# When to transpose the queries of a banded attention: four bursts at the group's begin, or one each two steps

## The chip, the core and the metric

One core of one Trainium2 chip runs the whole layer in a single launch. The metric is the device time in microseconds, the median over runs of the same program. TensorE (PE) does the matrix products and, as products with an identity, the transposes; VectorE (DVE) and ScalarE (ACT) do elementwise work and empty PSUM; GpSimd (POOL) and SyncE (SP) issue most of the DMAs.

## The reference

One layer of a decoder trunk: 256 tokens, width 2048, in float32. Two attentions run in parallel on the same normalized input, are gated and merged, and a gated feed-forward network with a short convolution follows. What matters here is the second attention, a banded one with 32 query heads of 64 columns and 4 key/value heads:

```python
s = jnp.einsum('bqhgd,bnkhd->bhgnqk', q, kb).astype(jnp.float32) * SWA_HEAD_DIM ** -0.5
...
s = jnp.where(mask[None, None, None], s + bias[None], -jnp.inf)
m = jnp.maximum(jnp.max(s, axis=-1), sink)
p = jnp.exp(s - m[..., None])
denom = jnp.sum(p, axis=-1) + jnp.exp(sink - m)
p = (p / denom[..., None]).astype(vb.dtype)
out = jnp.einsum('bhgnqk,bnkhd->bnqhgd', p, vb)
```

## The kernel before, in words

Products of float32 are made of three products of a high and a low part (`mm3`, lines 163 to 165). A weight chunk of 128 x 1024 is loaded by SP, ScalarE casts it into the high part (`whi`, line 137), VectorE subtracts to get the low part (`wlo`, line 138); up to four chunks of high and low parts are in store (`RING`), and three raw ones (`RAW`).

The big products run one after another (`gemm`, line 167). One of 512 columns takes eight chunks, with twelve matmuls of 512 columns each. After every chunk `tick()` runs the functions that were put down for that **step** with `at(step, f)`. So the attention is laid between the chunks of the products: a step is a chunk's twelve matmuls plus what was put down for it. The framework's scheduler then orders each engine's instructions with this order as the priority, and may move one later when it expects its inputs later.

The attention is cut into four **groups** (one for each key/value head, `g`) and 16 **units** of two query heads (`u`, four in a group). Group g's queries come out of one big product; group g is worked on while the next product runs. With b the first step of the group:

- `swa_q` (line 405) empties the product's two PSUM tiles into the query tiles `qx` (high and low part of each head side by side, lines 219 and 220). There are two such tiles, both used by one group.
- `swa_qT` (line 414) transposes a unit's queries: four 128 x 128 transposes on TensorE into one PSUM tile `xp` (line 420), copied by ScalarE to the tile `x2..` (line 423; the profile shows it as `x`; three buffers).
- `swa_unit` (line 433) puts down the unit's other steps, with t0 = b + 2 + 2i for unit i of the group: scores (`s`, lines 450 and 452) and their bias and maxima on VectorE (454 to 456) at t0; the exponentials on ScalarE (472) and the normalization, half on VectorE (484) and half on ScalarE (482), at t0 + 1; the transposes `pt` of the probabilities (430), emptied into `pth` by ScalarE (216) and `ptl` by VectorE (217), at t0 + 3; the product `po` with the values (498 to 501), emptied by ScalarE (503) and VectorE (506), at t0 + 4.

So in a running group a step holds either the scores of one unit and the `po` of an earlier one, or two `pt`. PSUM has eight banks: four for the big products (`pacc`), two for scores (`pss`) and two (`pst`) that `xp`, `pt`, `po` and, at the beginning, the key transposes `kt` take in turn:

```python
pst = ctx.enter_context(tc.tile_pool(name="pst", bufs=2, space=PS))
```

A tile of `pst` can be written only when the tile two before it in that pool has been emptied.

Of the kernel before, what the change touches and what calls it, by code (L numbers as in the profile page):

```python
# [41 lines left out]
def trunk_layer(ctx, tc, x, x_cols_in, conv_cols_in, g_mix_post, g_ffn_post, w_in, w_q, w_kv,  # L42
# [16 lines left out]
    def sb(pl, shape, name, dt=F32, tag=None, bufs=None):  # L59
        return pl.tile(shape, dt, name=name, tag=tag or name, **({"bufs": bufs} if bufs else {}))  # L60
# [84 lines left out]
    def at(t, *fs):  # L145
        steps[max(t, now[0])].extend(fs)
# [20 lines left out]
    def gemm(xh, xl, w, k0, nk, c0, n, split=False, extra=None, ps=None):  # L167

        kc = 1024 // n if n in (256, 512) else 2
        acc = new_acc("g", ps)  # L170
        todo = []
        cuts = list(range(0, nk, kc)) + [nk]
        for ci, (k, ke) in enumerate(zip(cuts[:-1], cuts[1:])):
            kk = ke - k
            src = w[(k0 + k) * P:(k0 + k + kk) * P, c0:c0 + n].rearrange("(a p) n -> p a n", p=P)
            hi, lo = wchunk(src, [kk, n], *(extra or {}).get(ci, ()))
            for j in range(kk):
                kt = k + j
                wh, wl = hi[:, j * n:(j + 1) * n], lo[:, j * n:(j + 1) * n]
                for t in range(NT):  # L180
                    def go(kt=kt, t=t, wh=wh, wl=wl):
                        mm3(acc[t][:, :n], xh(k0 + kt)[:, t * P:(t + 1) * P],
                            xl(k0 + kt)[:, t * P:(t + 1) * P], wh, wl, kt == 0, kt == nk - 1)
                    if split and t == 1:
                        todo.append(go)
                    else:
                        go()
            tick()
        return acc, todo
# [215 lines left out]
    def swa_q(g, acc):  # L405

        qx_of[g] = []
        for t in range(NT):
            q = sb(p1, [P, 8, 2, 64], f"qx{g}_{t}", F32R, tag="qx", bufs=2)
            a3 = acc[t].rearrange("p (a b) -> p a b", b=64)  # L410
            split_to(q[:, :, 0, :], q[:, :, 1, :], a3, r1s[:, t:t + 1])
            qx_of[g].append(q)

    def swa_qT(u):

        qx, i = qx_of[u // 4], u % 4
        pt = pst.tile([P, 512], F32R, name=f"xp{u}", tag="t")
        for j in range(2):
            for t in range(NT):
                pe.transpose(pt[:, (j * 2 + t) * P:(j * 2 + t + 1) * P],  # L420
                             qx[t][:, 2 * i + j, :, :].rearrange("p a b -> p (a b)"), ident_r)
        xt = sb(p1, [P, 512], f"x2{u}", F32R, tag="x2", bufs=3)
        act.copy(xt, pt.bitcast(F32))
        xs_of[u] = xt
# [91 lines left out]
    for g in range(4):  # L516
        acc = gemm(XH, XL, w_in, 0, KT, C_QS + 512 * g, 512)[0] if g else acc_q0
        swa_q(g, acc)
        b = now[0]
        for i in range(4):  # L520
            at(b + 1 + i // 2, lambda u=4 * g + i: swa_qT(u))
            swa_unit(4 * g + i, b + 2 + 2 * i)


# [235 lines left out]
    b = now[0] + 42  # L760
# [11 lines left out]
    for j in range(4):  # L772
        acc, _ = gemm(XH, XL, w_in, 0, KT, C_GA + 512 * j, 512)
        for t in range(NT):
            g = stg(f"ta{j}_{t}")
# [46 lines left out]
    for j in range(4):  # L822
        ld = merge_loads(j)
        acc, _ = gemm(AH, AL, wo_a, 0, KT, 512 * j, 512)
        for t in range(NT):
            a, b = ld[t]
# [354 lines left out]
```

## Time and profile before

| what | value |
|---|---|
| time before, median of 3 runs | 1485.88 us (1485.74 to 1486.16) |
| the profiled execution's own time | 1485.58 us |
| its span in the profile | 1483.8 us |
| granted TensorE clock, mean | 0.999 |
| transposes of the queries | 64 on TensorE, from 59.4 to 165.5 us |

The times of the profile count from the span's start. Between the span and the execution's own time lie 1.8 us that the profile does not show. An entry such as `PE xp L420 <- ACT x L423: 0.3, 2, 0.2` reads: TensorE's instruction of line 420, which writes xp, waited for ScalarE's instruction of line 423, which writes x; 0.3 us in total, two times, 0.2 us at the longest. In rows in order of time, the first number is the start, the second the duration, and the brackets at the end hold the idle time before and who ended it.

### The profile page before, as it was taken

To read this page: it belongs to the slowest core of one execution; us is meant where nothing else is said; L and a number is where in the kernel's file an instruction comes from. 1 tells how busy PE (TensorE), PEld (TensorE's weight loads), DVE (VectorE), ACT (ScalarE), POOL (GpSimd) and SP (SyncE) were. 2 spreads that over 40 slices of the span, in tenths; PEclk is the share of its full clock that TensorE was granted. 3 is DMA by queue.
4 is the path that set the end of the run, shared out by engine and by line. 5 is a ranking of instruction groups with operands and counts; after the bars stand their busy time and mean duration, and the time that the engine had idled before them with its cause. 6 is when DMAs were issued, how large, how long until landed. Compare 5 with 4: busy or idle time off the path is not lost.

```text
span 1483.8 us, 21178 instructions
## 1 busy us (share of the span) xinstructions
PE 1470.5 (99%) x7797; PEld 1261.1 (85%) x7797; DVE 979.3 (66%) x1711; ACT 806.3 (54%) x1336; POOL 57.0 (4%) x97
## 2 busy tenths in 40 slices
PE   9999999999999999999999999999999999999997
PEld 7888888888899988888888888888888888888887
DVE  7688884445677765555698777675444676677555
ACT  7588874434555554444566555554444555555443
POOL 0122200000000001000000000000000000000000
PEclk9999999999999999999999999999999999999999
DMA  9776566666655559656656666665566666665663
GB/s 306 206 170 175 137 198 187 208 209 206 185 157 157 167 160 334 225 185 213 197 178 176 199 191 178 196 191 190 190 194 198 187 187 193 188 188 185 195 197 114
DMA packets 162323, 285.52 MB, mean 192 GB/s; under 512 B 18555, under 2 KB 34844, under 8 KB 162092
## 3 DMA queue, kind: packets, MB, share of 16 engines
q1 hardware_dynamic: 157436, 268.39, 58.3%
q0 software_dynamic: 4784, 15.78, 4.5%
q8 instruction: 61, 1.00, 0.3%
q14 instruction: 42, 0.34, 0.1%
HBM read 277.79 MB, written 6.34 MB: 191 GB/s over the span
## 4 chain that ended last, share of the span: by engine, by line
PE 94%; DVE 3%; ACT 2%; issue 1%; DMA 0%; SPq 0%; DVEq 0%
PE accg L164 18%; PE accg L165 18%; PE accg L163 18%; PE ua L997 10%; PE ub L997 10%; PE ua L1001 5%; PE ub L1001 5%; PE mpo L748 1%; DVE wlo L138 1%; PE ms L714 1%; ACT p L472 1%; PE qn L677 1%; PE qn L679 1%; PE qn L678 1%; PE acckv L164 0%
## 5 line engine op out<-in xcount | busy, mean ns | idle before, releaser
L138 DVE TENSOR_TENSOR wlo<-raw,whi 128x1024 fp32r<-128x1024 f32 (+2 forms) x501 | 609.2, 1217 | 419.6 <-ACT whi L137 417.8
L137 ACT CAST whi<-raw 128x1024 fp32r<-128x1024 f32 (+2 forms) x501 | 523.2, 1046 | 547.0 <-PE accg L165 303.8
L163 PE MATMUL accg<-whi,bhl 128*128 128x512 f32 (+1 forms) x608 | 230.8, 380 | 0.0
L165 PE MATMUL accg<-whi,bhl 128*128 128x512 f32 (+1 forms) x608 | 230.1, 378 | 0.0
L164 PE MATMUL accg<-wlo,bhl 128*128 128x512 f32 (+1 forms) x608 | 230.0, 378 | 0.0
L163 PE MATMUL accg<-whi,ahl 128*128 128x512 f32 (+1 forms) x544 | 212.8, 391 | 0.0
L164 PE MATMUL accg<-wlo,ahl 128*128 128x512 f32 (+1 forms) x544 | 210.4, 387 | 0.0
L165 PE MATMUL accg<-whi,ahl 128*128 128x512 f32 (+1 forms) x544 | 210.1, 386 | 0.0
L997 PE MATMUL ub<-ahl,whi 128*128 128x512 f32 x640 | 160.3, 392 | 0.0
L997 PE MATMUL ua<-ahl,whi 128*128 128x512 f32 x640 | 160.2, 392 | 0.0
L997 PEld LDWEIGHTS ua<-ahl,whi 128*128 128x128 f32 x640 | 115.7, 189 | 21.1
L997 PEld LDWEIGHTS ub<-ahl,whi 128*128 128x128 f32 x640 | 115.6, 189 | 20.9
L165 PEld LDWEIGHTS accg<-whi,bhl 128*128 128x128 f32 x608 | 114.4, 188 | 21.2
L163 PEld LDWEIGHTS accg<-whi,bhl 128*128 128x128 f32 x608 | 114.4, 188 | 21.0
L164 PEld LDWEIGHTS accg<-wlo,bhl 128*128 128x128 f32 x608 | 114.4, 188 | 20.9
L165 PEld LDWEIGHTS accg<-whi,ahl 128*128 128x128 f32 x544 | 102.2, 188 | 20.3
L163 PEld LDWEIGHTS accg<-whi,ahl 128*128 128x128 f32 x544 | 102.3, 188 | 17.9
L164 PEld LDWEIGHTS accg<-wlo,ahl 128*128 128x128 f32 x544 | 102.3, 188 | 17.6
L1001 PEld LDWEIGHTS ub<-ahl,wlo 128*128 128x128 f32 x640 | 86.3, 191 | 5.6
L1001 PEld LDWEIGHTS ua<-ahl,wlo 128*128 128x128 f32 x640 | 86.0, 191 | 5.5
L1001 PE MATMUL ub<-ahl,wlo 128*128 128x256 f32 x640 | 88.0, 282 | 0.0
L1001 PE MATMUL ua<-ahl,wlo 128*128 128x256 f32 x640 | 87.9, 282 | 0.0
(331 smaller groups left out, 1617.6 us busy)
## 6 DMA issues: line engine op xcount, KB each, us to landing
raw<-in_ffn_w_up_dram SPq DMA_DIRECT2D x176, 512.0 KB, 4.5
raw<-in_w_in_dram SPq DMA_DIRECT2D x111, 512.0 KB, 4.5
raw<-in_ffn_w_down_dram SPq DMA_DIRECT2D x88, 512.0 KB, 3.8
raw<-in_w_o_swa_dram SPq DMA_DIRECT2D x32, 512.0 KB, 4.1
raw<-in_w_o_mla_dram SPq DMA_DIRECT2D x32, 512.0 KB, 4.7
raw<-in_w_out_dram SPq DMA_DIRECT2D x32, 512.0 KB, 4.2
raw<-in_mla_w_q_up_dram SPq DMA_DIRECT2D x48, 128.0 KB, 3.0
bias<-strip POOLq DMA_DIRECT2D x16, 256.0 KB, 4.1
```

Of the source, the lines that this page charges most:

```text
L137: act.copy(hi[:, :n], raw[:, :n])
L138: vec.tensor_tensor(lo[:, :n], raw[:, :n], hi[:, :n].bitcast(F32), op=ALU.subtract)
L163: pe.matmul(o, ah, bh, start=start, stop=False)
L164: pe.matmul(o, ah, bl, start=False, stop=False)
L165: pe.matmul(o, al, bh, start=False, stop=stop)
L472: act.activation(pb[:, i, a:b], pb[:, i, a:b], AF.Exp, bias=st["nm"][:, i, t:t + 1], accum_out=st["sm"][:, i, t:t + 1])
L677: pe.matmul(o, wh, ch(k), start=k == 0, stop=False)
L678: pe.matmul(o, wh, cl(k), start=False, stop=False)
L679: pe.matmul(o, wl, ch(k), start=False, stop=k == nk - 1)
L714: pe.matmul(o, w, v_, start=n == 0, stop=False)
L997: pe.matmul(acc[i], hi[:, c], hn[p][:, j * 512:(j + 1) * 512], start=p + j == 0, stop=stop)
L1001: pe.matmul(acc[i][:, 0:256], lo[:, c], hn[p][:, j * 512:j * 512 + 256], start=False, stop=False)
```

## The change

The query transposes of a group's four units are put down at the steps b + 1, b + 2, b + 4 and b + 6 in place of b + 1, b + 1, b + 2 and b + 2. The scores of the four units stay at b + 2, b + 4, b + 6 and b + 8.

```diff
         swa_q(g, acc)
         b = now[0]
         for i in range(4):
-            at(b + 1 + i // 2, lambda u=4 * g + i: swa_qT(u))
+            at(b + max(1, 2 * i), lambda u=4 * g + i: swa_qT(u))
             swa_unit(4 * g + i, b + 2 + 2 * i)
```

No instruction is added or removed. What stands on TensorE, in order, from the end of group 1 to the begin of group 2 in the two built programs (g12 are twelve matmuls of the big product; the numbers are units):

```
before  s7 g12 pt6 g9  xp8 g1 xp9 g2 po6 s8 xp10 g10 xp11 g6 pt7 g8 po7 s9 g12 pt8 g12 po8 s10
after   s7 g12 pt6 g11 xp8 g1 po6 s8 xp9 g12 pt7 g12 po7 s9 xp10 g12 pt8 g12 po8 s10 xp11
```

## The prediction

> **What bounds the kernel now.** I read the page first, then the answer for the tile xp (the transposed queries), then the waits of the stretch in which these transposes stand (52 to 212 us), then busy time by stretch, and last the instructions in order of time.
>
> ```profile
> PE 1470.5 (99%) x7797; PEld 1261.1 (85%) x7797; DVE 979.3 (66%) x1711; ACT 806.3 (54%) x1336; POOL 57.0 (4%) x97
> PE 94%; DVE 3%; ACT 2%; issue 1%; DMA 0%; SPq 0%; DVEq 0%
> ```
>
> TensorE is busy for 99% of the span and carries 94% of the chain that ended last. So only what TensorE waits for, or does in a costlier order, counts.
>
> ```profile
> L420 PE MATMUL xp<-ident_r,qx x64: 222/248/306, 59.4 to 165.5; 128*128 128x128 f32 x64
> L423 ACT CAST x<-xp x16: 565/587/603, 60.2 to 165.8; 128x512 fp32r<-128x512 f32 x16
> ```
>
> The 64 transposes are 16 bursts of four, each with one copy by ScalarE (0.59 us), all before 166 us. The built programs say how far the change reaches: on each engine the orders are the same up to the first burst and again from about 215 us on; the DMA queue of SP keeps its order throughout, and no instruction is added or dropped. So everything is decided in some 155 us of 1484, where TensorE waits this much:
>
> ```profile
> PE pt L430 <- ACT pth L216: 0.4, 1, 0.4
> PE xp L420 <- ACT x L423: 0.3, 2, 0.2
> PE cqT L550 <- DVE ptl L217: 0.3, 1, 0.3
> PE po L498 <- DVE ptl L217: 0.3, 1, 0.3
> PE xp L420 <- DVE ptl L217: 0.2, 1, 0.2
> ```
>
> That is 1.5 us in all. Its helpers are less at ease. In these two stretches (length; PE, PEld, DVE, ACT, POOL busy with counts; clock; DMA) VectorE has next to no idle time:
>
> ```profile
> 80.00:90.00 10.00, 10.00 (x55) 8.53 (x54) 9.91 (x32) 8.56 (x22) 2.34 (x3) 1.00 0.70 197
> 150.00:160.00 10.00, 10.00 (x54) 8.18 (x53) 9.86 (x30) 8.79 (x23) 3.88 (x6) 1.00 0.55 142
> ```
>
> **The waits that go.** A burst writes one of the two pst banks; the transposes of the probabilities (pt, two per unit) and the output products (po) use the same two. Before, steps 1 and 2 of a group ask for seven banks, later steps for one or two; after, every step asks for at most three. In the built program the second bursts of groups 2 and 3 (xp9, xp13), which wait 0.3 for a copy, move behind a unit's scores. And po4, which waits 0.3 because xp7 had pushed pt4 to within five products of it, gets a full step of twelve again. One wait grows: xp4, which stands twelve products behind pt2 and waits 0.2 for VectorE to empty its bank, now stands eleven behind it, so 0.2 more. Together 0.3 + 0.3 - 0.2 = 0.4 us. The other two waits belong to unit 14 and to the latent product, and stay.
>
> **What the place of a burst costs.** Two bursts in order of time, the first inside the big product, the second right behind a unit's scores, and then two products behind scores with no burst:
>
> ```profile
> 60.57 0.40 PE L163 MATMUL accg<-whi,ahl 128*128 128x512 f32 x1
> 60.85 0.53 PE L420 MATMUL xp<-ident_r,qx 128*128 128x128 f32 x4
> 61.22 0.47 PE L164 MATMUL accg<-wlo,ahl 128*128 128x512 f32 x1
> 61.52 0.39 PE L165 MATMUL accg<-whi,ahl 128*128 128x512 f32 x1
> ...
> 64.52 0.45 PE L420 MATMUL xp<-ident_r,qx 128*128 128x128 f32 x4
> 64.81 0.46 PE L163 MATMUL accg<-whi,ahl 128*128 128x512 f32 x1
> 65.11 0.40 PE L164 MATMUL accg<-wlo,ahl 128*128 128x512 f32 x1
> ...
> 72.88 0.39 PE L163 MATMUL accg<-whi,ahl 128*128 128x512 f32 x1
> 73.11 0.40 PE L164 MATMUL accg<-wlo,ahl 128*128 128x512 f32 x1
> ```
>
> By starts, a product takes 0.23 us. The burst alone takes TensorE from 60.80 (60.57 + 0.23) to 61.29 (61.52 - 0.23), 0.49 us; the one behind scores from 64.52 to 64.88, 0.36 us. So a place inside the product costs 0.13 us more: one switch in and one out, where the scores' own switch back is free (73.11 - 72.88 is 0.23). Before, ten runs of bursts stand inside the product or before a pt (xp1, xp3, xp4 with xp5, xp7, xp8, xp9, xp11, xp12, xp13, xp15); after, three (xp4, xp8, xp12, which wait for pt's bank and land one product ahead of po). Seven fewer at 0.13 give 0.9 us. Group 1 before also has pt3, pt4 and the scores of unit 5 cut in two by products or by po3; three such cuts, gone, at the same 0.13 give 0.4 us. The gain is 0.4 + 0.9 + 0.4 = 1.7 us; with the cuts free and no wait gone, 0.9; with xp4's wait gone as well, 2.1.
>
> The Trainium skill (TensorE: Matmul & The Clock Gate, Back-to-back issue gap) speaks against the 1.3 us of places: the spacing depends on the matmul's own columns, N / 2.4 + 2.5 ns, about 216 ns for 512, and names no cost of a switch. By it the gain would be the waits alone, 0.4 us. The rows above have 0.30 us between two products behind a burst and 0.23 elsewhere, so I go by the rows.
>
> **What becomes late.** In-order queues of ScalarE and VectorE are rearranged, and four things come near TensorE's need.
>
> First, units 5 and 9. Here is the end of a group before: ScalarE's normalization (L482) of unit 5, its share of the next queries (L219), and the transposes that need the former.
>
> ```profile
> 115.08 0.80 ACT L482 ACTIVATE p<-p,sm 128x128 f32<-128x128 f32 x2
> 116.20 1.27 ACT L219 ACTIVATE qx<-accg,r1s 128x512 fp32r<-128x512 f32 x2
> 116.53 0.82 PE L430 MATMUL pt<-ident,p 128*128 128x128 f32 x6
> ```
>
> After, ScalarE's queue has the copy of xp7, both L219, and only then L482. L219 needs the product's end, so L482 ends at 116.20 + 1.27 + 0.80 = 118.27. The pt of unit 5 now stands five products later; its second half, which needs L482, is due at 116.53 + 5 x 0.23 + 0.29 = 117.95. TensorE waits 0.3 to 0.4; for units 5 and 9, 0.7 us. If the queue ahead is late there, more; nothing excludes up to twice that.
>
> Second, units 3, 7 and 11, whose pt comes much sooner behind the scores of the next unit than before. The rows of unit 12's scores and unit 11's normalization:
>
> ```profile
> 161.02 1.05 ACT L137 CAST whi<-raw 128x1024 fp32r<-128x1024 f32 x1
> 161.53 0.28 PE L450 MATMUL s<-kx,x 128*128 128x256 f32 x1
> 163.58 1.22 DVE L138 TENSOR_TENSOR wlo<-raw,whi 128x1024 fp32r<-128x1024 f32 x1
> 165.32 0.42 DVE L506 TENSOR_TENSOR o<-po,cr 64x256 f32<-64x256 f32 x1
> 165.77 0.55 DVE L484 TENSOR_SCALAR p<-p,sm 128x128 f32<-128x128 f32 x2
> 167.03 0.82 PE L430 MATMUL pt<-ident,p 128*128 128x128 f32 x6
> ```
>
> Before, VectorE's normalization ends 4.79 us after the scores' start (166.32 - 161.53), and pt starts 5.50 after. After, pt is due at 0.70 (scores) + 0.36 (burst) + 0.07 + 12 x 0.23 = 3.9. But the order also puts the two weight splits, 1.05 us on ScalarE and 1.22 on VectorE, behind the normalization, which brings its end to 3.6 to 4.0. So the wait lies between nothing and 0.9 (4.79 - 3.9); I take 0.1, 0.3 for three.
>
> Third, the group's tail. The copy of xp15 (0.59) is new ahead of the casts of unit 13, and TensorE itself comes 0.36 later. po13 waits already (0.44 between these two where a product of 320 columns takes 0.15), and so does pt14 (0.4 above):
>
> ```profile
> 183.47 0.31 PE L165 MATMUL accg<-whi,ahl 128*128 128x320 f32 x1
> 183.91 0.47 PE L498 MATMUL po<-pth,vx 128*128 128x512 f32 x1
> ```
>
> I add 0.3 to each (between -0.3 and 0.59), 0.6.
>
> Fourth, xp4, xp8 and xp12 stand only one product and four po ahead of the scores that read them.
>
> ```profile
> 159.31 0.53 PE L420 MATMUL xp<-ident_r,qx 128*128 128x128 f32 x4
> 159.88 1.18 ACT L423 CAST x<-xp 128x512 fp32r<-128x512 f32 x2 [1.16 <-PE xp L420]
> ```
>
> The copy starts 0.57 behind the burst and takes 0.59, ready at 1.16; the scores are due at 0.38 + 0.30 + 0.69 = 1.37, with their weights loaded about 0.2 before. At 0.05 each, 0.2 in all; 0.1 each at most while ScalarE is idle, as here.
>
> The query tiles qx are held until step 6 instead of 2; the next group writes them after step 8, a step of 2.7 us later: nothing. The weights have up to four chunks in store, and their loads keep their order: nothing, and if that cover went, 0.3 a chunk.
>
> Late things add 0.7 + 0.3 + 0.6 + 0.2 = 1.8 us. The sum is 1.8 - 1.7 = +0.1 us on the profiled 1485.58, which is 0.3 below the median of the runs; on the median 1485.88 it gives 1486.0. The case's own range, with most ends not met at once, is -1.7 to +1.9: 1484.2 to 1487.8. A measurement of this kernel can tell about 0.2%, 3.0 us, from no change.
>
> **Rivals.** *The pair of banks becomes the wait at every unit (13%).* A burst now sits between po and the next pt, so pt's first half, not its second, needs po's bank, freed by the last half of L506.
>
> ```profile
> 180.65 0.42 DVE L506 TENSOR_TENSOR o<-po,cr 64x256 f32<-64x256 f32 x1
> 181.20 0.81 PE L430 MATMUL pt<-ident,p 128*128 128x128 f32 x6
> ```
>
> The slack here is 0.13 us (181.20 - 181.07), and a VectorE at 9.9 of 10 would eat the 0.43 that the burst adds. Twelve units have this. At 0.42 us each (one half of L506), 5.0 us: with the gain and the other late things (1.5), +4.8, 1490.7 us. It passes 0.2% from 0.27 us a unit ((3.0 + 1.7 - 1.5) / 12). Against it: the trace has pt waiting once in 16 units.
>
> *Nothing becomes late (10%).* Then -1.7 us, 1484.2. For it: the splits of the weights move out of the way of the normalizations, as in units 3, 7 and 11. Against it: L219 ahead of L482. This too is within 0.2%.
>
> *A switch costs the same everywhere (4%)*, as the page has it: 1.8 - 0.4 = +1.4, 1487.3 us. The rows speak against it.
>
> *The bursts don't move.* The step says only when an instruction is handed to the scheduler; but the built order shows 12 of 16 bursts behind a unit's scores, where 4 were, so no chance is given.
>
> **How the numbers follow.** Forecast 73%, rivals 13, 10 and 4%. Slower by over 0.2%: most of the first rival and a tail of the forecast with several ends met, 0.14. Faster by over 0.2% needs more than all the gain that I can find: 0.04. Within: 0.82. The range reaches past the forecast's own into the first rival's lower part and leaves out the rest of it: 1483.6 to 1488.6.
>
> **What would show it.** Right: a burst behind scores takes 0.36, no wait of xp but xp4's is left, pt of units 5 and 9 waits 0.3 to 0.4 for L482, and the stretch 59 to 215 us is within 2 us of its length. Wrong: pt waits for L506 at most units, whi or wlo ends waits of the product, or a stretch behind 215 us changes.

## The result: 2.6 us faster, and the profile after

After: 1483.10 us, median of 19 runs (1482.63 to 1485.10); before, on the same chip: 1485.67 us, 19 runs (1485.18 to 1486.16). The ratio is 0.9983, 95% interval 0.9977 to 0.9989: 2.6 us or 0.17% faster. The forecast was 1486.0 us with a range from 1483.6; the rival "nothing becomes late" (1484.2) came nearest. The prediction took 0.2% as the least that a measurement can tell; these 0.17% are clear, for the interval ends below 1. The profiled execution took 1483.36 us (before 1485.58), its span is 1481.6 us.

The page after, engines and the head of the chain:

```profile
PE 1469.5 (99%) x7797; PEld 1262.1 (85%) x7797; DVE 978.9 (66%) x1711; ACT 804.9 (54%) x1336; POOL 58.3 (4%) x97
PE 97%; DVE 1%; ACT 1%; DMA 0%; issue 0%; SPq 0%; DVEq 0%
```

The work is the same, and PE's share of the chain rose from 94 to 97%: VectorE and ScalarE ended fewer waits. The tile xp, and busy time in the two stretches shown for before:

```profile
L420 PE MATMUL xp<-ident_r,qx x64: 223/243/306, 59.7 to 176.7; 128*128 128x128 f32 x64
L423 ACT CAST x<-xp x16: 586/588/602, 60.5 to 178.5; 128x512 fp32r<-128x512 f32 x16
```

```profile
80.00:90.00 10.00, 10.00 (x56) 8.56 (x55) 9.70 (x30) 9.36 (x24) 2.58 (x3) 1.00 0.69 177
150.00:160.00 10.00, 10.00 (x56) 8.49 (x55) 8.77 (x28) 8.37 (x22) 2.52 (x4) 1.00 0.50 102
```

TensorE runs one or two matmuls more in the same ten microseconds, and VectorE fell from 9.86 to 8.77 in the second. In the list of TensorE's waits from 52 to 212 us, where before had five entries and 1.5 us, after has none. The prediction stopped at that list. A second list tells more: what the **weight loads** (PEld) waited for. Before, its first lines:

```profile
PEld xp L420 <- ACT x L423: 1.5, 3, 0.6
PEld xp L420 <- DVE ptl L217: 1.0, 2, 0.6
PEld po L498 <- issue: 1.0, 3, 0.6
...
```

and after:

```profile
PEld po L498 <- issue: 0.6, 2, 0.3
PEld xp L420 <- DVE ptl L217: 0.5, 1, 0.5
PEld pt L430 <- ACT qx L219: 0.5, 2, 0.2
...
```

Bursts whose loads waited for ScalarE's copy of x: three before, none after. In a running product a load stands about a product's time ahead of its matmul (in before one starts at 131.83 and its matmul at 132.06); one that comes late is no longer hidden, even where the matmul itself shows no wait. The row on which the prediction's price of a place rested, with its weight load beside it, in before:

```profile
60.84 0.39 PEld L420 LDWEIGHTS xp<-ident_r,qx 128*128 128x128 f32 x4 [0.32 <-ACT x L423]
60.85 0.53 PE L420 MATMUL xp<-ident_r,qx 128*128 128x128 f32 x4
```

and two bursts of after whose loads did not wait, the first inside the product, the second behind scores:

```profile
126.26 0.39 PE L164 MATMUL accg<-wlo,ahl 128*128 128x512 f32 x1
126.49 0.46 PE L420 MATMUL xp<-ident_r,qx 128*128 128x128 f32 x4
126.79 0.46 PE L165 MATMUL accg<-whi,ahl 128*128 128x512 f32 x1
127.09 0.39 PE L498 MATMUL po<-pth,vx 128*128 128x512 f32 x1
...
128.49 0.46 PE L420 MATMUL xp<-ident_r,qx 128*128 128x128 f32 x4
128.78 0.46 PE L163 MATMUL accg<-whi,ahl 128*128 128x512 f32 x1
129.08 0.40 PE L164 MATMUL accg<-wlo,ahl 128*128 128x512 f32 x1
```

Inside the product the burst adds 127.09 - 126.26 - 2 x 0.23 = 0.37 us; behind scores 129.08 - 128.49 - 0.23 = 0.36. The 0.49 of the prediction was a burst held up by a copy.

### An account by starts

TensorE's starts are measured, its ends modelled. So I add up, over all matmuls from 52.4 to 225 us, the time from one start to the next beyond the undisturbed pace of that shape (0.227 us for 512 columns, 0.147 for 320, 0.117 for 256, 0.097 for a transpose, 0.091 for one of xp's). The 0.091 is a quarter of the 0.36 that a burst adds. Before, the sum is 8.67 us, after 6.13. It comes from each kernel's one profiled execution; the medians and ratios come from all runs, each ratio against runs of before beside it. The same sum for the experiments that change only this stretch:

| kernel | median us | ratio to before, 95% interval | gaps by starts, us | median less gaps |
|---|---|---|---|---|
| before | 1485.67 | | 8.67 | 1477.0 |
| after | 1483.10 | 0.9983 (0.9977 to 0.9989) | 6.13 | 1477.0 |
| e1 group 1 | 1484.51 | 0.9992 (0.9983 to 1.0002) | 7.52 | 1477.0 |
| e2 groups 0, 2, 3 | 1484.05 | 0.9990 (0.9981 to 0.9999) | 7.12 | 1476.9 |
| e3 steps 0, 2, 4, 6 | 1484.17 | 0.9988 (0.9979 to 0.9997) | 7.25 | 1476.9 |
| e4 steps 1, 3, 5, 7 | 1485.47 | 0.9999 (0.9990 to 1.0008) | 8.55 | 1476.9 |
| e7 own banks, before | 1485.48 | 0.9998 (0.9989 to 1.0007) | 8.62 | 1476.9 |
| e8 own banks, after | 1484.16 | 0.9990 (0.9981 to 0.9998) | 7.47 | 1476.7 |
| e9 own banks, odd steps | 1485.92 | 1.0002 (0.9993 to 1.0011) | 8.87 | 1477.1 |
| e10 xp15 early | 1483.35 | 0.9986 (0.9977 to 0.9995) | 6.27 | 1477.1 |
| e11 GpSimd, before | 1487.05 | 1.0010 (1.0001 to 1.0019) | 10.06 | 1477.0 |
| e12 GpSimd, after | 1486.23 | 1.0004 (0.9995 to 1.0012) | 9.30 | 1476.9 |
| e13 two own banks, before | 1485.10 | 0.9996 (0.9987 to 1.0005) | 8.02 | 1477.1 |
| e14 one own bank, after | 1483.98 | 0.9989 (0.9980 to 0.9998) | 6.97 | 1477.0 |

The last column stays within 0.4 us while the times differ by 4: whatever these edits do to the time, they do by gaps of TensorE in this stretch. That is an account and not yet a cause: the matmuls are the same, so the sum of the gaps is the length of the stretch less a constant. It shows that the rest of the kernel keeps its length, and where the gaps lie. An interval reaches up to 1.4 us to either side, so differences of about 1 us between two of the variants are not shown by the times alone; the gaps put the variants in nearly the same order. By starts at equal content the gain of after lies in group 0 with 0.23 us, group 1 with 0.83, group 2 with 0.20, group 3 with 0.93 and the tail behind it with 0.34, together 2.5 us.

### The profile page after: what moved, and what is told of

The parts are those of the page before. It is cut to its first block, busy times and chain, and to the rows that moved or that the text cites. A ratio compares the mean times of both kernels' runs of the same rounds, so it can differ in the third digit from the quotient of the medians.

```text
span 1481.6 us, 21170 instructions
## 1 busy us (share of the span) xinstructions
PE 1469.5 (99%) x7797; PEld 1262.1 (85%) x7797; DVE 978.9 (66%) x1711; ACT 804.9 (54%) x1336; POOL 58.3 (4%) x97
## 4 chain that ended last, share of the span: by engine, by line
PE 97%; DVE 1%; ACT 1%; DMA 0%; issue 0%; SPq 0%; DVEq 0%
PE accg L163 18%; PE accg L165 18%; PE accg L164 18%; PE ua L997 10%; PE ub L997 10%; PE ua L1001 5%; PE ub L1001 5%; PE mpo L748 1%; PE ms L714 1%; PE pt L430 1%; PE qn L677 1%; PE qn L679 1%; PE qn L678 1%; PE acckv L164 0%; PE acckv L163 0%; PE accq L163 0%
```

## The experiments

My theory after the comparison: gaps that went, place by place, are the whole of it. Its rivals: the place of a burst is what costs (the prediction's 0.13 us); one disorderly spot was mended; the two shared banks are the one cause; VectorE's full queue is the one cause.

**e1 and e2: one part of the change alone.** The new steps in group 1 only, and in all other groups.

```diff
-            at(b + 1 + i // 2, lambda u=4 * g + i: swa_qT(u))
+            at(b + (max(1, 2 * i) if g == 1 else 1 + i // 2), lambda u=4 * g + i: swa_qT(u))   # e1
+            at(b + (max(1, 2 * i) if g != 1 else 1 + i // 2), lambda u=4 * g + i: swa_qT(u))   # e2
```

> The change in group 1 alone; the other three groups keep their query transposes at steps 1, 1, 2 and 2. If the gain adds up place by place (lost waits and fewer switches, with next to nothing becoming late), this keeps what the two traces show between the scores of units 3 and 7: 0.8 us of the 2.2 us, so 0.7 to 1.0 us below the kernel before. If the gain was only the repair of group 1, where the order before cut pt3, pt4 and the scores of unit 5 in two: nearly all of it, 2.0 to 2.5 us below. If it came from the stage's end: nothing, within 0.3 us.

> The change in groups 0, 2 and 3, with group 1 as before. Place by place: 1.2 to 1.8 us below the kernel before. Repair of group 1 alone: within 0.4 us of the kernel before. Stage's end: 2 us or more below.

1.1 us and 1.6 us below before (the interval of e1 reaches past 1; by gaps it is 1.15 and 1.55); the sum, 2.7, is about the gain of the whole, 2.6. So the gain adds up over the groups: group 1, the disorderly one, isn't all of it, nor is the tail.

**e3 and e4: the same spreading, other steps.** Steps 0, 2, 4, 6 (against after, only the first burst of a group moves, from between pt and po to behind the scores of the unit before), and steps 1, 3, 5, 7 (the first burst stays, the others move one step later).

```diff
-            at(b + 1 + i // 2, lambda u=4 * g + i: swa_qT(u))
+            at(b + (0, 2, 4, 6)[i], lambda u=4 * g + i: swa_qT(u))    # e3
+            at(b + (1, 3, 5, 7)[i], lambda u=4 * g + i: swa_qT(u))    # e4
```

> Steps 0, 2, 4 and 6 in place of 1, 2, 4 and 6: each group's first burst too stands right behind the scores of the unit before, and no burst stands inside the product any more. Place by place: below the changed kernel by the three lone bursts (0.13 us each), the wait of xp4 (0.3 us more than a product between the starts) and the waits in the middle of pt5 and pt9 (0.2 us each), 0.6 to 1.1 us. Rival, the first burst now comes before its query tiles are emptied by ScalarE and VectorE (0.7 and 0.75 us each, twice): TensorE waits up to 0.5 us in three groups, and it is 0.5 to 1.5 us above the changed kernel.

> The same spreading, one burst each two steps, but at steps 1, 3, 5 and 7, which hold the two pt of a unit, so that a burst asks for a third bank in the step where the two banks are wanted twice, and most bursts land inside the product. If the place decides (behind scores, with banks free): 1.0 to 2.5 us above the changed kernel, about the time before. If spreading as such helps: within 0.5 us of the changed kernel.

e3 is 1.1 us slower than after, where the theory had it faster; TensorE's waits in e3:

```profile
PE po L498 <- DVE ptl L217: 1.2, 4, 0.4
```

and in e4, which has the time of before:

```profile
PE xp L420 <- DVE ptl L217: 1.0, 2, 0.5
PE cqT L550 <- DVE cq L544: 0.3, 1, 0.3
PE pt L430 <- DVE p L484: 0.3, 1, 0.3
```

Spreading as such does not decide: with the first burst one step earlier, other waits take 1.1 of the 2.6 us, and with the other three one step later nearly all of it. Both are again told by the sum of gaps.

**e5 and e6: what a place costs, by itself.** Before, with 160 transposes of a constant added to the down projection, where no attention runs: 40 bursts of four, one behind each chunk, or ten runs of four bursts, one behind every fourth chunk.

```diff
+    def burst(i):
+        for q in range(1):                                   # e6: range(4)
+            pd = pst.tile([P, 512], F32R, name=f"dm{i}_{q}", tag="t")
+            for j in range(4):
+                pe.transpose(pd[:, j * P:(j + 1) * P], ident_r, ident_r)
+
+    for i in range(40):                                      # e6: range(10)
+        at(now[0] + 4 + 1 * i, lambda i=i: burst(i))         # e6: 4 * i
```

> The kernel before with 40 bursts of four transposes of a constant tile added, one behind each chunk of the first half of the down projection, into free banks, read by nobody. With 0.49 us for a burst inside the product (0.36 for the four and 0.13 for the switch in and out): 19.6 us above the kernel before. With no cost of a switch: 14.4 us.

> The same 160 transposes, but four bursts together behind every fourth chunk, so 10 places in place of 40. With the switch at 0.13 us: 14.4 + 1.3 = 15.7 us above the kernel before, 3.9 us less than with 40 places. With no cost of a switch: the same time as with 40 places, within 0.3 us.

1501.53 us (ratio 1.0107, interval 1.0089 to 1.0125) and 1500.09 us (1.0096, 1.0078 to 1.0114). The 30 places more cost 1.44 us, 0.048 each, where the prediction had 0.13; by starts at the bursts alone it is 0.98 us, 0.033 each. In order of time, a lone burst of e5 and a run of e6:

```profile
1024.55 0.40 PE L165 MATMUL accg<-whi,bhl 128*128 128x512 f32 x1
1024.78 0.46 PE L1048 MATMUL dm<-ident_r 128*128 128x128 f32 x4
1025.07 0.47 PE L163 MATMUL accg<-whi,bhl 128*128 128x512 f32 x1
1025.38 0.40 PE L164 MATMUL accg<-wlo,bhl 128*128 128x512 f32 x1
```

```profile
1024.92 1.50 PE L1048 MATMUL dm<-ident_r 128*128 128x128 f32 x16
1026.26 0.47 PE L163 MATMUL accg<-whi,bhl 128*128 128x512 f32 x1
1026.56 0.39 PE L164 MATMUL accg<-wlo,bhl 128*128 128x512 f32 x1
```

The product behind the transposes has its successor 0.30 us later instead of 0.23 (0.31 here in e5): that switch out, some 0.07, is there once a run, and it is there behind a burst that follows scores as well (128.78 to 129.08 above). So by these rows lone places inside the product and behind scores cost the same, and the prediction's term of 0.9 us has nothing under it.

**e7, e8, e9: other banks for the bursts.** The steps of before, of after and the odd ones, with xp in the pool of the scores.

```diff
-        pt = pst.tile([P, 512], F32R, name=f"xp{u}", tag="t")
+        pt = pss.tile([P, 512], F32R, name=f"xp{u}", tag="s")
```

> The bursts at the steps of before (1, 1, 2, 2), but their banks come from the pool of the scores, so the pair that pt and po use is left to these alone. If what the change took away were waits for that pair, weight loads held up by a copy of x or a split of pt included, then bringing the bursts no further and only giving them other banks gives most of it: 1.7 to 2.2 us below before, 1483.4 to 1484.0. If it were the places (0.13 us for each burst that stands inside the product), these stay, nine or ten of them, and only the 0.6 us of TensorE waits for xp and po4 can go: about 1485.0. A third way: the scores' two banks become the wait, 0.3 to 1 us for each group, and it is no faster than before.

> The bursts at the steps of after (1, 2, 4, 6), with banks from the pool of the scores. The built order has them four products behind the scores, inside the product, in place of right behind the scores. Waits for the pair of banks: xp4's (0.35 us) goes, nothing else changes, 1482.7 to 1483.2, so level with after or a little better. Places: twelve bursts more stand inside the product at 0.13, 1.6 us slower than after, about 1484.7.

> The odd steps (1, 3, 5, 7), which with the shared pair gave the time of before, now with banks from the pool of the scores. If the loss of the odd steps was the pair of banks (xp waited for the split of pt, six weight loads, 3.0 us of them), it goes: 1482.8 to 1483.5, level with after. If it was the queues of ScalarE and VectorE, which get the copies at the same late places, or the place behind pt, it stays at 1485 or so.

1485.48, 1484.16 and 1485.92 us: the pair of banks as the one cause falls. (The bursts now share the two banks of the scores, so this moves the sharing and doesn't end it; in e9 the longest wait is one of scores for a copy of x, 0.6 us.) e7 stays at before's time, with these waits in place of the old ones:

```profile
PE po L498 <- DVE ptl L217: 1.3, 3, 0.6
PE xp L420 <- DVE sm L478: 0.6, 2, 0.3
PE po L498 <- DVE cq_t L205: 0.4, 1, 0.4
PE cqT L550 <- DVE cq L544: 0.3, 1, 0.3
```

e8 loses 1.1 us against after. The number expected of the places, 1484.7, lay 0.5 off, but the trace has another cause: po3, po7 and po11 each wait for VectorE, and nothing else does. The last of VectorE's queue ahead of po7, and po7:

```profile
131.78 1.22 DVE L138 TENSOR_TENSOR wlo<-raw,whi 128x1024 fp32r<-128x1024 f32 x1
...
133.73 1.23 DVE L138 TENSOR_TENSOR wlo<-raw,whi 128x1024 fp32r<-128x1024 f32 x1
134.88 1.02 DVE L217 TENSOR_TENSOR ptl<-pt,pth 128x384 fp32r<-128x384 f32 x2
135.57 0.47 PE L498 MATMUL po<-pth,vx 128*128 128x512 f32 x1 [0.45 <-DVE ptl L217]
```

Here the split of pt (L217) stands behind two weight splits. In after, VectorE has one weight split between the maxima and L217, which starts at 133.52, 1.5 us ahead of its po at 135.02; nothing waits.

**e10: the tail.** After, but xp15 stays at step 2.

```diff
-            at(b + max(1, 2 * i), lambda u=4 * g + i: swa_qT(u))
+            at(b + (max(1, 2 * i) if i < 3 or g < 3 else 2), lambda u=4 * g + i: swa_qT(u))
```

> After, but the last burst (xp15) stays at step 2 of its group, seven products behind the scores of unit 12, and its copy leaves the tail. The prediction's step (the copy of x ahead of the casts of unit 13 costs po13 and pt14 0.3 us each) gives 0.3 to 0.6 us less than after, 1482.5 to 1482.8. If the tail gained in after because of what the order puts between there, as the trace shows it (po13 no longer waits, pt14 waits 0.25 less), the tail stays or goes back to before's: as after, or 0.3 to 0.5 us more, 1483.1 to 1483.6, with xp15 or pt11 waiting for the bank now and then.

1483.35 us, as after. The copy of xp15 in the tail costs nothing that can be measured; without it the waits there only sit elsewhere (po14 0.4 and the latent product's transpose 0.3, by TensorE's waits).

**e11 and e12: VectorE relieved.** Half the normalization to GpSimd, on before's and on after's steps.

```diff
-                        vec.tensor_scalar(pb[:, i, a:b], pb[:, i, a:b], sm[:, i, t:t + 1], None, op0=ALU.mult)
+                        pool.tensor_scalar(pb[:, i, a:b], pb[:, i, a:b], sm[:, i, t:t + 1], None, op0=ALU.mult)
```

> Before, with the first half of the normalization (L484, two instructions a unit, 10.2 us in all on VectorE) given to GpSimd, which is idle there. If the waits come from VectorE's queue (the split of pt, L217, stands behind weight splits and normalization, and the copy-and-split chain gives the banks back late), they go although the bursts stay at steps 1 and 2: 1.5 to 2.5 us below before, 1483.1 to 1484.1. If it is the two banks asked for by bursts standing close together, the waits of xp for the copy of x stay (xp9, xp13, xp4 and xp5, 1.3 us and what hangs on them): 1484.6 to 1485.5. Third: GpSimd takes longer over the normalization than VectorE did (its 128x256 subtraction, L508, takes 0.93 us), pt waits for it, and it is slower than before.

> After, with the same half of the normalization given to GpSimd. VectorE's queue: little is left to win, the waits of pt in units 5 and 9 and xp4's at most (0.8 us), and before and after come within 0.7 us of each other: 1482.3 to 1483.2. The two banks: it stays 1.5 to 2.5 us below the same edit on before. Third, as there: pt waits for GpSimd and both are slower by the same.

1487.05 and 1486.23 us: both above before (the interval of e12 holds 1), and after's lead shrinks to 0.8 us. The waits in e12; e11 has the first two as well, with 2.0 and 1.6:

```profile
PE xp L420 <- DVE ptl L217: 2.5, 3, 0.9
PE pt L430 <- POOL p L484: 1.6, 1, 1.6
PE po L500 <- DVE ptl L217: 0.2, 1, 0.2
```

The scheduler, with other expectations of the engines, puts xp4, xp8 and xp12 ten products behind pt instead of eleven, and each waits 0.8 to 0.9 us for the split of pt, which nothing expected; one pt waits 1.6 us for GpSimd, as the third expectation had it. As a test of VectorE's queue the pair is inconclusive, since it changed the order too.

**e13 and e14: other banks only for the bursts that wait.** Before with xp of a group's first two units in the scores' pool; after with that of the first unit.

```diff
-        pt = pst.tile([P, 512], F32R, name=f"xp{u}", tag="t")
+        pt = (pss if u % 4 < 2 else pst).tile([P, 512], F32R, name=f"xp{u}", tag="s" if u % 4 < 2 else "t")     # e13
+        pt = (pss if u % 4 == 0 else pst).tile([P, 512], F32R, name=f"xp{u}", tag="s" if u % 4 == 0 else "t")   # e14
```

> Before, with banks from the scores' pool for the first two bursts of a group alone, which stand in step 1, before the next scores; the other two keep the pair. Their built order has xp8 and xp9 together behind pt and no burst waiting for a copy of x. If waits of the bursts for the pair (xp4 with xp5 0.55, xp9 0.39, xp13 0.41 by starts, and po4 0.41) are most of what the change took away, this gives most of it without spreading anything: 1483.3 to 1484.2. If the waits only move to po, which needs the split of pt from VectorE (as with all four bursts in the scores' banks, 1485.48), it is 1484.8 to 1485.6.

> After, with the first burst of each group in a bank of the scores' pool; it then stands right behind pt, and the wait of xp4 for the split of pt has nothing left to wait on. Waits: 0.35 us less for xp4, 0.2 to 0.4 more for pt4 and pt7, which the new order cuts in two by products: 1482.7 to 1483.3. If the pair is not what holds xp4 but VectorE being late, po4 or po3 waits instead: 1483.1 to 1483.8.

1485.10 us, 0.4 below before in place of 1.3 to 2.2, with its interval across 1; and 1483.98, 0.9 above after. The expectation of e13 calls the bursts that wait for a copy xp9 and xp13. By the order on TensorE they are xp11 and xp15, which keep the pair here and wait 0.17 us each as before; so e13 tries other banks only for xp4 with xp5. These two wait no more, but xp7 now waits 0.61. In e14 po3, po4 and po7 wait in place of xp4:

```profile
PE xp L420 <- ACT x L423: 0.9, 3, 0.6
```

```profile
PE po L498 <- DVE ptl L217: 1.0, 3, 0.6
```

No variant beat after.

## Why the prediction was wrong

It added 1.7 us of gains to 1.8 us of things that become late. Of its signs of being right, two came out: a burst behind scores takes 0.36 us, and of the waits of xp only xp4's is left (0.34 by starts). The stretch changed by 2.5 us, where it named 2 as the most. Point by point, by starts:

- **The waits that go: 0.4 expected, 1.7 measured.** This is the first step that failed. Its mechanism is right: the waits of before are gone. Its size came from the idle column, which counts from the modelled end of the matmul ahead. The prediction's xp9 in before:

```profile
132.06 0.39 PE L163 MATMUL accg<-whi,ahl 128*128 128x512 f32 x1
132.60 0.39 PEld L420 LDWEIGHTS xp<-ident_r,qx 128*128 128x128 f32 x4 [0.58 <-ACT x L423]
132.61 0.53 PE L420 MATMUL xp<-ident_r,qx 128*128 128x128 f32 x4 [0.16 <-ACT x L423]
132.97 0.47 PE L164 MATMUL accg<-wlo,ahl 128*128 128x512 f32 x1
```

  By the order it is xp11, as xp13 is xp15. It had 0.16 in the idle column. By starts it had 0.55 behind a product that takes 0.23, so 0.32, and its four transposes took 0.36 where undisturbed ones take 0.29: 0.39 in all. Four more places showed no TensorE wait at all, or a small one, and were held up: those at 60.85 and 65.61 by 0.12 and 0.08, xp4 with xp5 by 0.55, xp12 by 0.21. With the fourth bursts of groups 2 and 3 at 0.39 and 0.41 that makes 1.76; xp4 after keeps 0.34. So 1.4 for bursts, and 0.3 for po4, which came to 0.41 before and 0.10 after. The Trainium skill (Perfetto Trace Analysis, Tensor Engine Instruction) says that the profiler estimates a matmul's end from its size and that TensorE can pull weight loads ahead of matmuls in flight; the 0.16 in the idle column beside 0.32 by starts, and the loads at 60.84 and 132.60 us that came only after the copy, agree.
- **The place of a burst: 0.9 expected, nothing measured.** The second step that failed. The pattern row had a hidden wait for the copy of xp0 in it; without one, a burst adds 0.37 us inside the product and 0.36 behind scores, and e5 against e6 has 0.048 for a place. The Trainium skill (TensorE: Matmul & The Clock Gate, Back-to-back issue gap) gives the formula that the prediction took from it for an isolated matmul only, says that in a stream the weight load and the matmul both set the spacing, and names no cost of a switch; as a difference between the two kinds of place the runs agree with it, as an absolute they do not (0.07 us behind a run of transposes). So the condition of the prediction's rival of 4%, the same cost everywhere, was met; its 1487.3 us came out wrong by the other terms.
- **Cuts in group 1: 0.4 expected, about 0.6 measured** (0.18 at pt3, 0.17 at pt4, and 0.26 where po3 cut the scores of unit 5 and its first load came late).
- **Units 5 and 9: 0.7 expected, 0.4 measured,** of which 0.3 is new. The order came out as forecast, L482 behind both L219:

```profile
115.03 1.37 ACT L219 ACTIVATE qx<-accg,r1s 128x512 fp32r<-128x512 f32 x2
116.29 0.79 ACT L482 ACTIVATE p<-p,sm 128x128 f32<-128x128 f32 x2
116.62 0.31 PEld L430 LDWEIGHTS pt<-ident,p 128*128 128x128 f32 x3 [0.24 <-ACT qx L219]
116.65 1.04 PE L430 MATMUL pt<-ident,p 128*128 128x128 f32 x6
117.13 0.31 PEld L430 LDWEIGHTS pt<-ident,p 128*128 128x128 f32 x3 [0.20 <-ACT p L482]
```

  This is the after kernel; pt takes 0.79 from its start to the next product (117.44) where six transposes take 0.58.
- **Units 3, 7 and 11: 0.3 expected, nothing measured.** Unit 11 in after: scores, copy of x, both halves of the normalization, pt.

```profile
159.97 0.28 PE L450 MATMUL s<-kx,x 128*128 128x256 f32 x1
...
162.67 0.60 DVE L484 TENSOR_SCALAR p<-p,sm 128x128 f32<-128x128 f32 x2
162.74 0.80 ACT L482 ACTIVATE p<-p,sm 128x128 f32<-128x128 f32 x2
163.78 0.82 PE L430 MATMUL pt<-ident,p 128*128 128x128 f32 x6
```

  The normalization ends 3.3 us (VectorE) and 3.6 us (ScalarE) behind the scores' start, pt stands 3.8 behind: the weight splits did move out of its way, by more than the 3.6 to 4.0 of the prediction allowed for.
- **The tail: 0.6 more expected, about 0.6 less measured.** The third step that failed, with the wrong sign. po13 had 0.29 of gap and has none, pt14 goes from 0.54 to 0.29, the latent product's transpose from 0.47 to 0.26, against 0.2 more at po14. The casts of unit 13, before and then after:

```profile
182.69 0.86 ACT L216 CAST pth<-pt 128x384 fp32r<-128x384 f32 x2
```

```profile
180.67 0.84 ACT L216 CAST pth<-pt 128x384 fp32r<-128x384 f32 x2
```

  After they start 1.4 us ahead of po13 (182.07); before they started 0.9 ahead of the 183.62 at which po13 was due. ScalarE had more ahead of them, not less: the copy of xp15 (0.59), one half of L536 (0.69) and its sum L537 (0.60) where before had both halves of L536 (1.26). But it came to this work earlier: the normalization L482 ended 1.2 us ahead of pt13 (178.50 and 179.66), before 0.2 (180.97 and 181.20). The prediction added the new copy to a queue that it left where it was. VectorE's split of pt13 lies earlier too; which of the two decides isn't shown. e10 shows that where the copy of xp15 stands doesn't decide.
- **Copies of xp4, xp8 and xp12: 0.2 expected, none measured.** Their scores start without a gap (1.29 us behind the burst at 158.68).

Together -1.7 - 0.6 + 0.3 - 0.6 = -2.6 us, as measured (2.5 by starts); the forecast had +0.1.

The first rival, the pair of banks at every unit, did not come: no pt waits for L506. In e3, one step earlier, po waits four times, but for the split of pt (L217).

**What stays open.** Shown is that the gain is made of single gaps of 0.1 to 0.55 us, in all groups and the tail. Not shown is one cause behind them. Other banks and other steps removed waits that they aimed at and made others; less work on VectorE left waits for its split of pt and changed the order. In each variant the scheduler writes the queues anew, so none of them tests one cause alone. Why after's order, of all, leaves the splits and copies in time is only read from its trace (one weight split ahead of L217, not two); an order with just that one exchange wasn't tried.

## What to carry to other kernels

Price a stall of a saturated TensorE by the starts of its matmuls, with the weight loads' waits beside them; before taking a cost from one pair of rows, look whether the load of that very instruction waited. Where several in-order engines share a stretch and a scheduler orders them, a change of a step is a new order of all queues: read in the built order what each queue gains and also what it loses, and expect that one step beside a good one part or all of the gain can be lost.

## What was not expected of the hardware

A burst of four transposes whose first weight load came late took 0.36 to 0.38 us by starts, one whose loads ran ahead 0.29. And 16 transposes in a row took 1.34 us (e6), 0.084 each; each has a weight load of its own. The Trainium skill (TensorE: Matmul & The Clock Gate, Back-to-back issue gap) has about 81 ns for a matmul of 128 columns in a stream of weight loads and matmuls, which makes 1.30 us as an estimate: the trace agrees, where the formula of the prediction, about 56 ns, would give 0.89. For 512 columns the same sentence has about 131 ns, and there it differs: the products here take 0.227 us each, and the measurement decides.
